# GpSimd hands weights' low parts, norm differences, residual sums, S5, rope and decay products to VectorE

## The chip, the cores and the metric

The kernel runs on one core of one Trainium2 chip. The core has TensorE (PE; its weight loads are listed as PEld), VectorE (DVE), ScalarE (ACT), GpSimd (POOL), and SyncE (SP), whose queue issues the DMAs. The metric is the device time of one execution in microseconds, as the median of several runs. TensorE's granted clock is given by the profile as a share of its upper level of 2.4 GHz; the lower level is 1.2 GHz.

## The reference

Two layers of a block over 1024 latent tokens and 256 context tokens of width 1024. In each layer the tokens are normalised and modulated, projected by one wide matrix into the columns of four mixers and their gates, mixed, gated, projected back and added to the stream. Cut to what matters here:

```python
for l in range(DEPTH):
    h = rmsnorm(x, g_pre[l]) * (1.0 + scale[:, None]) + shift[:, None]
    hc = rmsnorm(xc, g_pre[l]) * (1.0 + scale_c) + shift_c
    p_kv, p_q = jnp.split(h @ w_in[l], [N_CTX_COLS], axis=-1)
    ...
    y_gla, yc_gla = gla_mixer(...)      # linear attention with decays; rope on q and k
    y_na, yc_na = na_mixer(...)         # attention in an 8 x 16 window of a 2-D grid, and to the context
    y_s5, yc_s5 = s5_mixer(...)         # 16 groups of a diagonal state space model, two directions
    y_pool = pool_mixer(...)            # centred means over 2, 4, 8, 16 tokens
    y = jnp.concatenate([y_gla, y_na, y_s5, y_pool], axis=-1) * jax.nn.silu(gate_cols)
    x = x + gate[:, None] * rmsnorm(y @ w_out[l], g_post[l])
    # the context tokens likewise, except in the last layer
```

All of it is in float32.

## The kernel before

**Products in two parts.** TensorE gets each float32 operand as a high part (rounded) and a low part (the rest). `load_w` (L289) makes them for weights: a DMA brings a block of 128 x 1024 into the tile `w`, ScalarE rounds it into `wh` (L302), and another engine subtracts, `wl = w - wh` (L303). `norm_turn` (L268) does the same for the normalised tokens: `ahi` (L286) and `alo` (L287); `out_load` (L366) for the gated mixer outputs (L378 the gating, L381 the difference). Each product then is three series of matmuls: high by high, high by low, low by high. The weights' tiles lie in pools of three high parts, three low parts and two raw blocks, so a low part may be written only when the matmuls that read the tile three blocks ago are done. The output weights have tiles of their own (`wx`).

**Stages of a layer.** `norm_turn` prepares the tokens; `proj_tok` (L324, matmuls at L334) and `proj_cols` (L308, matmuls at L318) project them. `proj_gates` (L339) calls `proj_cols` for the output gates, applies a tanh and a product and stores the result in DRAM (L349). `s5_params` (L508) builds the state space matrices: per pair of groups complex products of 128 x 256 tiles, each made of products (L512 and, through `gmul`, L513) with a difference (L514) or a sum (L515); transposes by TensorE at L651 and small products at L656 and L657 read the results `sp_zr` and `sp_zi`, and `sp_R` is stored at L660. `gla_prep` (L862) rotates q and k (rope: a shuffle L893, a product with the sine L894, with the cosine L895, the sum L896), computes the decay gates (TensorE L901, VectorE L903), and sums them up (L915). `gla` (L990) subtracts the chunk's middle from the sums (L1001), clips (L1002), multiplies, reduces the largest decay to `glmx` (L1008), which TensorE transposes (L1010), and compares it with a limit (L1013). A branch on that flag (L1555) then takes the form with factored decays, which is the one that is run here; the other form never runs. The neighbourhood attention `na` (products L1315 and L1382, softmax L1322 to L1330), the pooling (L1434 to L1460) and the linear attention follow. Last comes the output: `out_load`, `out_mm` (matmuls L388), the squares, and `out_finish` (L447): the scaled rows (L474), the residual sum (L475), and, for the next layer's norm, a square with sum on ScalarE (L482) and the scaling (L483). The reciprocal root between them (L132 to L140) runs on VectorE.

**What sets the order.** Each engine runs its instructions in one fixed order. A scheduler sets it at build time by priorities and by the data each step needs, with its own idea of durations. The projections of the gates and of the pooling have low priority, so they fill TensorE's gaps; they stand on both sides of the branch, and what the scheduler has placed ahead of it can't fill behind it.

**Who does what.** A string `ENG` of 13 digits says for 13 kinds of elementwise work whether VectorE (1) or GpSimd (0) does it; `self.eng(i)` returns the engine.

## Time and profile before

| | us |
|---|---|
| median of 3 runs | 1439.78 |
| lowest, highest | 1434.55, 1441.52 |
| the profiled execution | 1441.78 |
| its span, first to last instruction | 1440.0 |
| TensorE busy | 1286.8 |
| VectorE busy | 898.0 |
| ScalarE busy | 585.0 |
| GpSimd busy | 414.0 |

The mean granted clock over the span is 0.951. The profiled execution lies 2.0 us above the median of the runs, and 1.8 us of it are outside the span. Busy time counts how long an engine had an instruction under way, also where that instruction was held up by another engine; so a busy share says nothing by itself about whether the engine could have done more. What bounds a stage is read from the waits: which engine stood idle, and whose result came last. Times within the span are counted from its first instruction. S5's products of layer 0 run from about 119 to 162 us, the output products of layer 0 come from about 690 on; S5's products of layer 1 are under way at 866, and the output products of layer 1 fill the time from 1380 on.

### The profile page before, as it was taken

What the parts mean: (1) busy time and instruction counts of PE and PEld (TensorE: products, weight loads), DVE (VectorE), ACT (ScalarE), POOL (GpSimd) and SP (SyncE); (2) the same over time, 40 slices, a digit from 0 to 9 for tenths busy, and PEclk for the clock granted to TensorE, in tenths of its full rate; (3) what the DMA queues carried; (4) which work ended last, traced back from release to release, by engine and by line L of the source; (5) the groups of instructions that cost most, each with busy time, mean ns of one, the idle gap of its engine ahead of it and who ended that gap; (6) DMA issues with size and microseconds to landing.
All of it is one profiled execution on the core that took longest, in us unless ns stands there. A gap on an engine that the chain in (4) does not pass through costs nothing. (4 is left out here: it accounts for less than half of the span.)

```text
span 1440.0 us, 20173 instructions
## 1 busy us (share of the span) xinstructions
PE 1286.8 (89%) x6958; PEld 1025.7 (71%) x6958; DVE 898.0 (62%) x2113; ACT 585.0 (41%) x1218; POOL 414.0 (29%) x368
## 2 busy tenths in 40 slices
PE   5798988999999899989999898888989989977897
PEld 2687956567777688767778877856867766765676
DVE  2878576555378557844654578385553894776473
ACT  2642433222333346733455642442233323665321
POOL 0215342010101033432654536331121110234351
PEclk9798999999999999989999998989999999988999
DMA  9445674762533277726842374655324535755662
GB/s 333 144 125 182 210 214 137 211 178 64 178 116 115 91 202 179 208 87 210 241 130 92 113 215 163 205 169 143 107 77 158 156 125 150 196 158 163 180 205 90
DMA packets 223479, 231.09 MB, mean 160 GB/s; under 512 B 47016, under 2 KB 176552, under 8 KB 223040
## 3 DMA queue, kind: packets, MB, share of 16 engines
q1 hardware_dynamic: 221776, 227.14, 52.3%
q10 hardware_dynamic: 1584, 2.49, 0.5%
q8 instruction: 59, 0.97, 0.3%
q14 instruction: 60, 0.49, 0.1%
HBM read 159.97 MB, written 69.62 MB: 159 GB/s over the span
## 5 line engine op out<-in xcount | busy, mean ns | idle before, releaser
L303 POOL TENSOR_TENSOR wl<-w,wh 128x1024 fp32r<-128x1024 f32 (+1 forms) x45 | 118.1, 2632 | 437.6 <-PE pa L318 197.1
L318 PE MATMUL pa<-ahi,wh 128*128 128x512 f32 (+1 forms) x664 | 175.2, 392 | 5.5 <-DVE stg L856 2.5
L318 PE MATMUL pa<-ahi,wl 128*128 128x512 f32 (+1 forms) x664 | 171.1, 385 | 0.4 <-PEq L1555 0.4
L318 PE MATMUL pa<-alo,wh 128*128 128x512 f32 (+1 forms) x664 | 168.2, 380 | 0.1
L318 PEld LDWEIGHTS pa<-ahi,wh 128*128 128x128 f32 x664 | 119.2, 198 | 34.5 <-issue 8.4
L318 PEld LDWEIGHTS pa<-ahi,wl 128*128 128x128 f32 x664 | 117.1, 195 | 28.9 <-issue 11.3
L318 PEld LDWEIGHTS pa<-alo,wh 128*128 128x128 f32 x664 | 115.8, 194 | 25.5 <-issue 7.5
L334 PE MATMUL pa<-wh,ahi 128*128 128x256 f32 (+1 forms) x480 | 84.8, 311 | 6.3 <-ACT wh L302 2.4
L388 PE MATMUL po<-wx,ahi 128*128 128x512 f32 x312 | 82.8, 407 | 4.8 <-ACT ahi L380 2.6
L334 PE MATMUL pa<-wl,ahi 128*128 128x256 f32 (+1 forms) x480 | 81.5, 304 | 2.5 <-POOL wl L303 2.5
L334 PEld LDWEIGHTS pa<-wh,ahi 128*128 128x128 f32 x480 | 70.2, 201 | 14.2 <-issue 5.4
L334 PE MATMUL pa<-wh,alo 128*128 128x256 f32 (+1 forms) x480 | 78.2, 300 | 0.0
L302 ACT CAST wh<-w 128x1024 fp32r<-128x1024 f32 (+1 forms) x51 | 53.7, 1056 | 57.3 <-PE pa L318 34.9
L1315 PE MATMUL nS<-naK,naQ 128*128 128x256 f32 (+2 forms) x256 | 58.8, 349 | 19.8 <-DVE nast L1322 17.3
L388 PEld LDWEIGHTS po<-wx,ahi 128*128 128x128 f32 x312 | 61.1, 197 | 19.5 <-ACT ahi L380 3.5
L334 PEld LDWEIGHTS pa<-wl,ahi 128*128 128x128 f32 x480 | 69.2, 199 | 5.8 <-POOL wl L303 3.0
L334 PEld LDWEIGHTS pa<-wh,alo 128*128 128x128 f32 x480 | 67.9, 197 | 1.7 <-issue 1.4
L1322 DVE CUSTOM_DVE_ANT_0 naP<-nS,nab 128x640 f32<-128x640 f32 (+1 forms) x64 | 50.2, 785 | 28.9 <-ACT nab L1273 14.8
L1315 PEld LDWEIGHTS nS<-naK,naQ 128*128 128x128 f32 x256 | 45.0, 204 | 32.0 <-DVE nast L1322 26.2
L198 PE MATMUL pm<-wm,csil 128*32 128x512 f32 x192 | 47.8, 679 | 19.0 <-DVE nr2v L132 9.5
L973 POOL TENSOR_TENSOR qs<-QB,ind 128x512 f32<-128x512 f32 x18 | 18.8, 1047 | 148.4 <-PE pb L1062 144.3
L1327 ACT ACTIVATE naP<-naP,nast 128x640 f32<-128x640 f32 (+1 forms) x64 | 51.5, 804 | 22.8 <-DVE nast L1322 17.5
(395 smaller groups left out, 2735.2 us busy)
## 6 DMA issues: line engine op xcount, KB each, us to landing
wm<-in_w_mod_dram SPq DMA_DIRECT2D x48, 512.0 KB
w<-in_w_in_dram SPq DMA_DIRECT2D x41, 512.0 KB
s5R<-dR SPq DMA_DIRECT2D x16, 960.0 KB
xt<-in_tok_dram SPq DMA_DIRECT2D x20, 512.0 KB
dR<-sp_R SPq DMA_DIRECT2D x16, 512.0 KB
dG<-stg SPq DMA_DIRECT2D x32, 256.0 KB
w<-in_w_out_dram SPq DMA_DIRECT2D x16, 512.0 KB
naQ<-dQ SPq DMA_DIRECT2D x24, 320.0 KB
```

Of the source, the lines that this page charges most:

```text
L198: nc.tensor.matmul(state[0][32 * k:32 * k + 32, :], lhsT=self.csil[:, (k0 + k) // 2, 2 * (k % 2):2 * (k % 2) + 32], rhs=ws[k // 2][:, k % ...
L302: nc.scalar.copy(hi, raw)
L303: (next(engines) if engines else self.eng(2)).tensor_tensor(lo, raw, hi.bitcast(F32), ALU.subtract)
L318: nc.tensor.matmul(ps[:, :t1 - t0], lhsT=w(k), rhs=x[:, k, t0:t1], start=(i == 0), stop=(i == 23))
L334: nc.tensor.matmul(ps[:, :n], lhsT=x[:, k, t * 128:(t + 1) * 128], rhs=w(k), start=(i == 0), stop=(i == 23))
L388: self.nc.tensor.matmul(o, lhsT=x[:, k], rhs=m(k), start=first and i == 0, stop=last and i == len(todo) - 1)
L973: (nc.gpsimd if BD[d] == "p" else nc.vector).tensor_tensor(out, Q.unsqueeze(1).to_broadcast(sh), ind.unsqueeze(2).to_broadcast(sh), ALU.mult)
L1315: nc.tensor.matmul(ps[:, c * 128:(c + n) * 128], lhsT=Qb[:, i, :], rhs=K[:, b * 128:(b + n) * 128], start=(i == 0), stop=(i == 1))
L1322: v.tensor_tensor_reduce(P[:, 0:nk], ps, bias[:, b0:b0 + nk], 1.0, -NEG, ALU.add, ALU.min, nm)
L1327: nc.scalar.activation(P[:, 0:nk], src, AF.Exp, bias=nm, scale=-1.0, accum_out=l1)
```

## The change

Six digits of `ENG` turn from 0 to 1: index 1 (the norm's `alo`, L287), 2 (the low parts of the weights, L303), 5 (the residual sum, L475), 6 (S5's `gmul`, L513), 10 (rope's sine product, L894) and 11 (the decay differences, L1001). `proj_cols` gets an argument with engines for `load_w`, and `proj_gates` passes GpSimd without end, so the low parts of the gates' weights stay there. Some low parts at the start of the program have had GpSimd or VectorE named for them before and are as they were.

```diff
-ENG = '0001000101001'
+ENG = '0111011101111'
...
-    def proj_cols(self, l, c0, n, evac, chunks, scale=None, psum=None):
+    def proj_cols(self, l, c0, n, evac, chunks, scale=None, psum=None, engines=None):
...
-            hi, lo = self.load_w(self.a["w_in"][l][:, c0 + m * 128:c0 + (m + 1) * 128], 128, scale=scale)
+            hi, lo = self.load_w(self.a["w_in"][l][:, c0 + m * 128:c0 + (m + 1) * 128], 128, scale=scale, engines=engines)
...
-        self.proj_cols(l, 1824 + m0 * 128, 128, evac, chunks, psum=psum)
+        self.proj_cols(l, 1824 + m0 * 128, 128, evac, chunks, psum=psum, engines=itertools.repeat(nc.gpsimd))
```

Of the instructions that are run, 156 move: 26 low parts of weights (24 of 128 x 1024, two of 128 x 1152), 20 norm differences, 34 residual sums, 64 products of S5, 8 of rope, 4 decay differences. VectorE's program has 3253 rows before and 3417 now, GpSimd's 555 and 391; eight of the 164 are rope products in the form that isn't run. The scheduler lays all engines' orders anew. Three places:

VectorE in S5 of layer 0, before. L512 is a product on VectorE, L514 and L515 the difference and the sum with a product `sp_big` that GpSimd makes.

```order
L512 TENSOR_TENSOR sp_zi_1290<-sp_zpr_1239,sp_bbi_1230 128x256
L512 TENSOR_TENSOR sp_R_1288<-sp_c2r_1263,sp_wpr_1241 128x2x128
L514 TENSOR_TENSOR sp_zi_1290<-sp_zi_1290,sp_big_1295 128x256
L514 TENSOR_TENSOR sp_R_1288<-sp_R_1288,sp_big_1299 128x2x128
L512 TENSOR_TENSOR sp_R_1288<-sp_c2i_1264,sp_wpr_1241 128x2x128
L515 TENSOR_TENSOR sp_R_1288<-sp_R_1288,sp_big_1300 128x2x128
L512 TENSOR_TENSOR sp_zr_1321<-sp_zpr_1239,sp_bbr_1229 128x256
L512 TENSOR_TENSOR sp_zi_1322<-sp_zpr_1239,sp_bbi_1230 128x256
```


VectorE at the same place, now:

```order
L513 TENSOR_TENSOR sp_big_1280<-sp_c2i_1264,sp_wpi_1242 128x256
L512 TENSOR_TENSOR sp_R_1269<-sp_c2i_1264,sp_wpr_1241 128x2x128
L514 TENSOR_TENSOR sp_R_1269<-sp_R_1269,sp_big_1280 128x2x128
L513 TENSOR_TENSOR sp_big_1281<-sp_c2r_1263,sp_wpi_1242 128x256
L512 TENSOR_TENSOR sp_zr_1289<-sp_zpr_1239,sp_bbr_1229 128x256
L515 TENSOR_TENSOR sp_R_1269<-sp_R_1269,sp_big_1281 128x2x128
L513 TENSOR_TENSOR sp_big_1291<-sp_zpi_1240,sp_bbi_1230 128x256
L512 TENSOR_TENSOR sp_zi_1290<-sp_zpr_1239,sp_bbi_1230 128x256
```


The products at L513 stand between the others, each ahead of the sum or difference that needs it.

VectorE at the end of S5 of layer 0 and ahead of the rope (L893), before. L1200 writes attention queries and keys.

```order
L515 TENSOR_TENSOR sp_R_1480<-sp_R_1480,sp_big_1492 128x2x128
L512 TENSOR_TENSOR sp_X_1532<-sp_i_321_1534,sp_dd_1089 16x256
L514 TENSOR_TENSOR sp_kc_1088<-sp_kc_1088,sp_X_1532 16x256
L514 TENSOR_TENSOR sp_T_320_1533<-sp_T_1530,sp_T_1531 128x2048
L1200 TENSOR_TENSOR stn_2795<-pa_2770,stn_2795 128x256
L893 STREAM_SHUFFLE QF_1560<-glk_1568 128x512
L893 STREAM_SHUFFLE KF_1561<-glq_1569 128x512
L1200 TENSOR_TENSOR stn_2833<-pa_2808,stn_2833 128x8x8x8
```


VectorE at the same place, now (`wl` is a low part; the fourth, `wl_3099`, gets the buffer of the first):

```order
L515 TENSOR_TENSOR sp_R_1480<-sp_R_1480,sp_big_1492 128x2x128
L303 TENSOR_TENSOR wl_2765<-w_2766,wh_2764 128x1024
L512 TENSOR_TENSOR sp_X_1532<-sp_i_321_1534,sp_dd_1089 16x256
L514 TENSOR_TENSOR sp_kc_1088<-sp_kc_1088,sp_X_1532 16x256
L303 TENSOR_TENSOR wl_2873<-w_2874,wh_2872 128x1024
L303 TENSOR_TENSOR wl_2979<-w_2980,wh_2978 128x1024
L1200 TENSOR_TENSOR stn_2795<-pa_2770,stn_2795 128x256
L514 TENSOR_TENSOR sp_T_320_1533<-sp_T_1530,sp_T_1531 128x2048
L1200 TENSOR_TENSOR stn_2833<-pa_2808,stn_2833 128x8x8x8
L303 TENSOR_TENSOR wl_3099<-w_3100,wh_3098 128x1024
L1200 TENSOR_TENSOR stn_2865<-pa_2840,stn_2865 128x8x8x8
L893 STREAM_SHUFFLE QF_1560<-glk_1568 128x512
```


Four low parts have come ahead of the first rope instruction.

TensorE at the end of the neighbourhood attention of layer 0 (its last product L1382) and ahead of the output products (L388), before. The L318 rows are gates' and other projections.

```order
L1382 MATMUL nT_9631<-naPT_9601,naV_9107 128x256 x3
L318 MATMUL pa_8229<-ahi,wl_8195 128x512 x8
L318 MATMUL pa_8258<-ahi,wh_8194 128x512 x8
L318 MATMUL pa_8258<-alo,wh_8194 128x512 x8
L318 MATMUL pa_8258<-ahi,wl_8195 128x512 x8
L318 MATMUL pa_8293<-ahi,wh_8287 128x256 x8
L318 MATMUL pa_8293<-alo,wh_8287 128x256 x8
L318 MATMUL pa_8293<-ahi,wl_8288 128x256 x8
L318 MATMUL pa_8322<-ahi,wh_8287 128x512 x8
L318 MATMUL pa_8322<-alo,wh_8287 128x512 x8
L318 MATMUL pa_8322<-ahi,wl_8288 128x512 x8
L318 MATMUL pa_9671<-ahi,wh_9665 128x512 x8
```


TensorE at the same place, now:

```order
L1382 MATMUL nT_9631<-naPT_9601,naV_9107 128x256 x3
L318 MATMUL pa_8322<-alo,wh_8287 128x512
L318 MATMUL pa_8322<-ahi,wl_8288 128x512 x8
L318 MATMUL pa_9671<-ahi,wh_9665 128x512 x8
L318 MATMUL pa_9671<-alo,wh_9665 128x512 x8
L318 MATMUL pa_9671<-ahi,wl_9666 128x512 x8
L388 MATMUL pa_9748<-wh_9710,stn_9499 128x512 x2
```


Of L318, 104 matmuls (24 with 256 columns) stood there and 33 stand now. The others have moved up: ahead of the branch of layer 0 there are 854 matmuls of L318 for 813 before, between it and the first attention product (L1315) 70 for 59, within the attention 195 for 176. In layer 1 it is 787 for 730 from the end of layer 0's attention to the branch, 53 for 49 behind it, and none for 61 within the attention.

## Rows read from the trace of the kernel before

**Rows 1.** The page's first part: busy us of each engine, share, instructions.

```profile
PE 1286.8 (89%) x6958; PEld 1025.7 (71%) x6958; DVE 898.0 (62%) x2113; ACT 585.0 (41%) x1218; POOL 414.0 (29%) x368
```

**Rows 2.** Waits of TensorE: line waiting <- line waited for: us, times, longest.

```profile
PE pb L651 <- DVE sp_zr L515: 11.0, 7, 4.0
...
PE pb L1010 <- DVE glmx L1008: 9.0, 2, 4.7
PE po L388 <- DVE stg L474: 8.5, 4, 3.2
...
PE pb L901 <- DVE QF L903: 3.5, 1, 3.5
...
PE pa L334 <- POOL wl L303: 2.5, 2, 1.8
```

**Rows 3.** Timeline in S5 of layer 0: start, us, engine, line, operation, [idle before].

```profile
130.48 2.52 POOL L303 TENSOR_TENSOR wl<-w,wh 128x1024 fp32r<-128x1024 f32 x1
130.72 2.56 DVE L515 TENSOR_TENSOR sp_zr<-sp_zr,sp_big 128x256 f32<-128x256 f32 x1
133.20 0.41 DVE L514 TENSOR_TENSOR sp_zi<-sp_zi,sp_big 128x256 f32<-128x256 f32 x1
...
133.42 0.45 PE L651 MATMUL pb<-c_ident,sp_zr 128*128 128x128 f32 x1 [3.60 <-DVE sp_zr L515]
```

**Rows 4.** Windows of 10 us: length, busy us of each engine, clock, DMA share, GB/s.

```profile
130.00:140.00 10.00, 6.58 (x31) 6.61 (x32) 8.21 (x12) 1.89 (x3) 4.49 (x4) 0.58 0.38 131
710.00:720.00 10.00, 6.89 (x26) 5.43 (x25) 7.81 (x22) 4.38 (x9) 6.83 (x6) 0.76 0.71 205
870.00:880.00 10.00, 6.42 (x34) 6.42 (x35) 8.28 (x11) 1.40 (x2) 4.73 (x5) 0.55 0.32 106
930.00:940.00 10.00, 3.93 (x18) 1.77 (x16) 8.80 (x11) 0.33 (x1) 5.68 (x3) 0.68 0.66 173
940.00:950.00 10.00, 8.83 (x30) 7.04 (x32) 8.46 (x15) 6.06 (x6) 2.52 (x2) 0.63 0.61 179
970.00:980.00 10.00, 5.64 (x23) 2.21 (x21) 7.25 (x10) 4.29 (x6) 0.00 (x0) 0.73 0.52 140
```

**Rows 5.** GpSimd by form: line, operation, tiles, count, busy, mean ns, idle before.

```profile
L303 POOL TENSOR_TENSOR wl<-w,wh 128x1024 fp32r<-128x1024 f32 x41 | 107.6, 2630 | 401.5 <-PE pa L318 197.1 <-ACT wh L302 149.3 <-DVE s5st L772 28.9
L475 POOL TENSOR_TENSOR xt<-xt,stg 128x512 f32<-128x512 f32 x34 | 45.4, 1356 | 46.3 <-DVE stg L474 37.9 <-issue 8.3
...
L287 POOL TENSOR_TENSOR alo<-nh,ahi 128x512 fp32r<-128x512 f32 x20 | 26.0, 1305 | 26.7 <-DVE ahi L286 23.6 <-DVE ry L140 2.3 <-DVE rv L132 0.4
...
L513 POOL TENSOR_TENSOR sp_big<-sp_zpi,sp_bbi 128x256 f32<-128x256 f32 x16 | 12.4, 778 | 25.9 <-DVE sp_R L514 19.6 <-DVE sp_bbi L514 6.3
...
L1001 POOL TENSOR_TENSOR QF<-glPF 128x1280 f32<-128x1280 f32 x2 | 6.0, 3014 | 19.8 <-DVE glPF L915 19.8
```

**Rows 6.** VectorE by form, the same columns.

```profile
L515 DVE TENSOR_TENSOR sp_zr<-sp_zr,sp_big 128x256 f32<-128x256 f32 x16 | 14.2, 885 | 2.6 <-POOL sp_big L513 2.6
...
L303 DVE TENSOR_TENSOR wl<-w,wh 128x1024 fp32r<-128x1024 f32 x6 | 7.3, 1218 | 9.1 <-PE pa L318 8.9 <-ACT wh L302 0.2
...
L265 DVE TENSOR_TENSOR alo<-nh,ahi 128x512 fp32r<-128x512 f32 x8 | 5.2, 685 | 0.1
```

**Rows 7.** Waits of the low parts on GpSimd and on VectorE.

```profile
POOL wl L303 <- PE pa L318: 197.1, 14, 33.6
...
DVE wx L303 <- ACT wx L302: 14.6, 8, 2.7
...
DVE wl L303 <- PE pa L318: 8.9, 2, 4.6
```

**Rows 8.** Timeline at an output turn of layer 0: residual sums, then the square.

```profile
706.04 3.04 POOL L475 TENSOR_TENSOR xt<-xt,stg 128x512 f32<-128x512 f32 x2
...
709.12 1.06 ACT L482 ACTIVATE stn<-xt 128x1024 f32<-128x1024 f32 x1 [2.38 <-POOL xt L475]
```

**Rows 9.** The chain that ended last: start, us, line, number.

```profile
1380.72 50.87 PE po L388 x216
```


## The prediction

> **What bounds the kernel now.** I read the page's first line, then TensorE's waits, then the windows with its granted clock, then the instructions of GpSimd and VectorE by form. The first line [rows 1] says that TensorE (PE) is busy for 1286.8 of the 1440.0 us of the span, VectorE (DVE) for 898.0 and GpSimd (POOL) for 414.0. So TensorE bounds the kernel, with some 153 us of idle time, and the change can only win a part of that idle time, and the time that TensorE spends at a low clock. Work taken off GpSimd is worth nothing by itself.
>
> Which of TensorE's waits end at something that the change touches? Five lines do [rows 2]: the S5 transposes at L651 waiting for a product that needs one of GpSimd's (11.0 us in 7 waits), the GLA transposes at L1010 waiting behind the decay differences (9.0 in 2), the output products at L388 (8.5 in 4), the gate products at L901 (3.5), and L334 waiting for a low part (2.5). Together 34.5 us. The others (DMA, the softmax of the neighbourhood attention) are not touched.
>
> Why is L651 late? [rows 3] shows it: GpSimd starts a low part of 2.52 us at 130.48, VectorE's product sp_zr starts at 130.72 and takes 2.56 us, though the like product right behind it takes 0.41, and the TensorE transpose that needs it has waited 3.60 us. Both end together: VectorE's two-operand product stood still while GpSimd's ran. The windows [rows 4] show the second price: after such waits the granted clock is lower, 0.58 at 130 to 140 and 0.55 at 870 to 880 (S5 of the two layers), 0.68, 0.63 and 0.73 around GLA of layer 1, 0.76 at an output wait. Between the levels of 1.2 and 2.4 GHz, a mean of 0.58 with 6.58 us busy means that about (1 - 0.58) x 6.58 = 2.8 us of work at full clock was not done. The six rows give 2.8 + 2.9 (S5), 1.3 + 3.3 + 1.5 (GLA), and 1.7 (output) us: 13.5 in all.
>
> **What is moved, and its bare cost.** From GpSimd go 26 low parts of weights at 2.63 us, 34 residual sums at 1.36, 20 norm differences at 1.31, 64 S5 products at 0.78, 4 decay differences at 3.0 [rows 5], and 8 rope products, which have the size of the norm differences: about 68 + 46 + 26 + 50 + 12 + 10 = 212 us of its 414. On VectorE a low part takes 1.22 and a 128x512 difference 0.685 [rows 6], a 128x256 product 0.41 when nothing is beside it [rows 3]; the decay difference is estimated by size, 1280/512 x 0.685 = 1.71. So it gets 26 x 1.22 + 64 x 0.41 + 62 x 0.685 + 4 x 1.71 = 107 us, and wins back some of what it lost beside GpSimd: 16 products at L515 at 0.885 [rows 6] instead of 0.41 are 8 us. It comes to about 1000 us, 69% of the span, below TensorE: in the mean VectorE does not become the bound. In a stretch it may.
>
> **(a) S5 products: -13.** Per pair of groups, VectorE issues a product, waits for GpSimd's, and adds. On one engine there is no hand-over and no product standing still: four 0.41 instead of four 0.78 on another engine. Bounds: 0 if the transposes find another late input, and 11.0 + 5.7 (clock) = 16.7 if all goes. I take 9 of 11.0, since one or two of the seven waits are likely to come from the loop's own length, which VectorE now carries alone, and 4 of 5.7 with them.
>
> **(b) Decay differences and rope: -12.** The order moves output-gate products of TensorE ahead of the branch: in layer 0, 41 matmuls of 512 columns, in layer 1, 57. In the steady part at the end 216 such take 50.87 us [rows 9], 0.236 each, so 9.7 and 13.5 us of work now stand where TensorE waited 9.0 us in two waits. Those waits should go (-9). On VectorE itself the chain is about as long as before: the eight rope products and four differences add 8 x 0.685 + 4 x 1.71 = 12.3 us to it, but no hand-over and no standing still are left. Of L901's 3.5 and the clock's 6.1 I take 3. Bounds: 0 (the chain grows by what it wins) and 18.6.
>
> **(c) Residual, norm, weights in the output stage: -6.** At an output turn two residual sums take 3.04 us on GpSimd, the square on ScalarE (L482) waits 2.38 us for them [rows 8], and VectorE, in order, waits for that square with the next tile's scaling behind it, for which L388 waits. Two sums on VectorE are 1.37 us, 1.7 less, for each of the four waits of 8.5: some 4 of them, as a shorter wait leaves its rest. L334's 2.5 for a low part: 2 go. Bounds: 0 and 8.5 + 2.5 + 1.7 = 12.7.
>
> **(d) Cover given back: +8.** The gate products that fill the waits in (b) are the ones that stood elsewhere. Behind the last attention product of layer 0 there were 104 (24 of them half as wide), now 33: 71 x 0.236 = 17 us less to do while the attention's last tiles are normalised, stored and read back for the output stage. The attention of layer 1 keeps none of the 61 it had. What of the 17 us was needed there no row tells; bounds are 0 and 17, and I take the middle.
>
> **(e) Low parts on the in-order VectorE: +4.** A low part waits for the cast on ScalarE and for the buffer that TensorE frees. On GpSimd such waits were free: 197.1 us in 14 for the buffer [rows 7]. On VectorE everything behind waits too. The rows that show it there are the output weights (14.6 us in 8, 1.8 each) and 8.9 in 2 for a buffer. Bounds: 0 if all falls into VectorE's slack (TensorE waited for no VectorE low part so far), and 26 x 1.8 = 47 if all reaches TensorE. I take one wait of the longer kind (4.5), rounded to 4, since VectorE has 440 us of slack.
>
> Sum: -13 - 12 - 6 + 8 + 4 = -19. On the profiled execution, 1441.8, this gives 1422.8; that execution lies 2.0 above the median of 1439.8, so **1421** is forecast.
>
> **Rivals.** *The standing still remains (no change).* GpSimd keeps 17 low parts of the gates, the gating products of the output stage and the pooling; a moved product that starts beside one of these stands still as in [rows 3], 2.56 - 0.41 = 2.15 us at a low part. If each of the 17 meets one, and half of it reaches TensorE, that is 17 x 2.15 / 2 = 18 us: 1439. For it: the gates' low parts are filler, spread over just these stretches. Against it: in (a) and (b) VectorE no longer waits for GpSimd's result itself. The Trainium skill, SBUF — State Buffer, "Who interferes with whom", says that the two engines share a port pair by an exclusive lock, so that the later one stops fully, whichever it is; it speaks for this rival, and the trace agrees (2.56 beside 0.41 us).
>
> *VectorE's queue blocks (slower).* Place: ahead of the rope in both layers. In the new order four low parts, the last with the buffer that the first must leave, stand ahead of the first rope instruction. If that buffer is still being read, VectorE waits with rope, scans and differences behind it. The mean wait for such a buffer was 197.1 / 14 = 14.1 us [rows 7]. If the whole of it is exposed in both layers, 28 us come on top, (b)'s 12 are not won, and the cover's loss is 17, not 8: 1422.8 + 28 + 12 + 9 - 2 = 1470; with half the wait exposed, 1456. It outweighs the gains once over (19 - 12) / 2 = 3.5 us per layer are exposed. Against it: the fill that frees the buffer also keeps TensorE busy until then. The Trainium skill, TensorE: Matmul & The Clock Gate (its opening table), lists VectorE's queue as strictly first in, first out; the trace agrees, since the waits on VectorE in [rows 7] let nothing pass.
>
> *All of it goes (faster still).* All five waits and the lost clock, with nothing given back: 1441.8 - 34.5 - 13.5 - 2 = 1392.
>
> That the change does less than it says is excluded: the order has 164 rows more on VectorE and as many less on GpSimd.
>
> **How the numbers follow.** Forecast (1405 to 1433) 0.55; no change (1433 to 1447) 0.18; slower (about 1447 to 1470) 0.15; faster still (1392 to 1405) 0.12. A run of this kernel can be told from no change at about 0.5%, 7 us. So faster 0.66 (the forecast and the last, less a little of the forecast's edge), same 0.19, slower 0.15. The range of 1392 to 1452 leaves out most of the blocked queue and little else.
>
> **What would show it.** (a) the line L651 <- sp_zr falls below 3 us, and the clock at S5 in both layers stays above 0.9; products at L512 and L515 take about 0.41. (b) L1010 <- glmx falls to near nothing; if the line grows, the queue blocks. (c) L388 <- stg halves. (d) a new TensorE wait between the attention of layer 0 and its output products, or in the attention of layer 1. (e) new lines "wl L303 <- PE" on VectorE, and TensorE waiting for VectorE low parts. I am wrong if TensorE's busy time at full clock changes by more than a few us, or if the gain is in stages where no row above has a wait.

## The result and the profile after

The changed kernel takes 1390.53 us in the median (1389.38 to 1392.13, 4 runs); the kernel before took 1440.65 beside it. The ratio is 0.9653, with a 95% interval of 0.9627 to 0.9679: 50 us faster, where 19 were forecast, and 1.5 us below the lower end of the range of 1392 to 1452. For the kernel below with the weights back, median and ratio are of seven executions, without three of 1444 to 1446 us that lie over 1.5% above its fastest; a loss of 44 us that an expectation names for it is from the median of all ten.

The first part of the page, after (engine, busy us, share of the span, instructions), beside [rows 1]:

```profile
span 1388.7 us, 20066 instructions
...
PE 1265.2 (91%) x6958; PEld 1011.0 (73%) x6958; DVE 912.5 (66%) x2269; ACT 584.9 (42%) x1218; POOL 203.8 (15%) x212
```

Three numbers here tell the case. TensorE has the same 6958 matmuls, but is busy for 1265.2 us and not 1286.8: 21.6 us less, which is the clock (its mean went from 0.951 to 0.968). Its idle time, span less busy, went from 153.2 to 123.5: 29.7 us less. The two are the 51.3 us by which the span got shorter. And GpSimd's busy time fell by 210.2 us, close to the 212 that the prediction had moved, but VectorE's rose by 14.5 us only, from 898.0 to 912.5, though 156 instructions came to it.

What these instructions take on VectorE, from the same kernel's rows by form (line, operation, tiles, count, then busy us and mean ns of one):

```profile
L303 DVE TENSOR_TENSOR wl<-w,wh 128x1024 fp32r<-128x1024 f32 x30 | 37.2, 1242 | 27.7 <-ACT wh L302 17.4 <-PE pa L318 10.3
...
L303 DVE TENSOR_TENSOR wl<-w,wh 128x1152 fp32r<-128x1152 f32 x2 | 2.6, 1356 | 2.2 <-ACT wh L302 2.2
...
L475 DVE TENSOR_TENSOR xt<-xt,stg 128x512 f32<-128x512 f32 x34 | 25.2, 780 | 0.0
...
L287 DVE TENSOR_TENSOR alo<-nh,ahi 128x512 fp32r<-128x512 f32 x20 | 13.8, 691 | 1.2
...
L381 DVE TENSOR_TENSOR alo<-yt,ahi 128x512 fp32r<-128x512 f32 x24 | 20.2, 847 | 11.9 <-ACT ahi L380 11.5
...
L286 DVE CAST ahi<-nh 128x512 fp32r<-128x512 f32 x20 | 8.5, 425 | 11.1 <-ACT nh L280 11.1
...
L513 DVE TENSOR_TENSOR sp_big<-sp_zpi,sp_bbi 128x256 f32<-128x256 f32 x16 | 6.6, 414 | 0.1
...
L515 DVE TENSOR_TENSOR sp_zr<-sp_zr,sp_big 128x256 f32<-128x256 f32 x16 | 6.6, 413 | 0.0
...
L1001 DVE TENSOR_TENSOR QF<-glPF 128x1280 f32<-128x1280 f32 x2 | 2.9, 1472 | 0.0
...
L894 DVE TENSOR_TENSOR QF<-QF,rs 128x512 f32<-128x512 f32 x4 | 2.8, 690 | 0.5 <-DMA rs<-in_rope_s_dram 0.5
```

Low parts: 37.2 less the 7.3 of the six that were there before [rows 6], and 2.6 for two of 128x1152, are 32.5. Residual sums 25.2, norm 13.8, the four forms of L513 6.6 each, rope 5.6, decay 5.9: 109.4 us in all, for 107 predicted. So 898.0 + 109.4 - 912.5 = 94.9 us of VectorE's busy time have gone. Most of that was no work: the durations of the 2113 instructions that VectorE had before add up to 84.4 us less now. The other 10.5 us come from the way of counting, since the records of neighbouring instructions overlap by some 45 ns each, and a new one adds less than its duration. L515's 16 sums take 413 ns and not 885 [rows 6]; and operations that the change does not touch got shorter in the same way. Before, by form:

```profile
L381 DVE TENSOR_TENSOR alo<-yt,ahi 128x512 fp32r<-128x512 f32 x24 | 23.0, 959 | 19.2 <-ACT ahi L380 18.7
...
L140 DVE SCALAR_TENSOR_TENSOR ry<-rw,ry 128x1 f32<-128x1 f32 x84 | 21.6, 270 | 1.1
...
L286 DVE CAST ahi<-nh 128x512 fp32r<-128x512 f32 x20 | 16.1, 811 | 14.7 <-ACT nh L280 14.7
...
L895 DVE TENSOR_TENSOR glq<-glq,rc 128x512 f32<-128x512 f32 x4 | 5.9, 1486 | 0.0
```

L381 went from 959 to 847 ns, L286 from 811 to 425; of the other two, after:

```profile
L140 DVE SCALAR_TENSOR_TENSOR ry<-rw,ry 128x1 f32<-128x1 f32 x84 | 14.7, 183 | 1.0
...
L895 DVE TENSOR_TENSOR glq<-glq,rc 128x512 f32<-128x512 f32 x4 | 2.8, 690 | 0.0
```

L140 works on one number per partition and L895 on 512. The trace before shows beside what they were long. Of L140's 84 executions, the 31 that overlap an operation of GpSimd (fills not counted) took 466 ns on the mean, the other 53 took 155 and none over 160. For L895 it is 1557 ns (6) and 680 (2), and for the cast L286, which has one operand only, 1067 (12) and 426 (8). The product ahead of L140, with one tile and two numbers per partition as operands (`rw`, L136), is not drawn out: 270 ns (30) and 269 (54). So a good part of VectorE's work stood still while GpSimd worked, though not all kinds of it.

TensorE's waits after (us, times, longest), to hold beside [rows 2]:

```profile
PE po L388 <- DVE stg L474: 6.3, 4, 3.7
...
PE pb L901 <- DVE QF L903: 2.2, 1, 2.2
...
PE pm L198 <- DMA wm<-in_w_mod_dram: 0.8, 2, 0.7
...
PE pb L651 <- DVE sp_zi L514: 0.7, 1, 0.7
...
PE pb L1010 <- DVE glmx L1008: 0.6, 2, 0.3
```

L651's 11.0 us are 0.7 (for the other product), L1010's 9.0 are 0.6, L901's 3.5 are 2.2, L388's 8.5 are 6.3, and L334's line for the low part on GpSimd is gone. One line went that was not counted, of before:

```profile
PE pm L198 <- DMA wm<-in_w_mod_dram: 9.5, 3, 4.5
```

The waits for the modulation's weights went from 9.5 to 0.8 us. Between S5's last transposes and the first L198, TensorE's order has 123 matmuls of L318 now and had 65 (131 and 87 in layer 1), so it comes to L198 with more done, when the data have landed. No run tests that by itself.

By stage, windows of before: S5 of layer 0, then from S5's end to L1010 (rope and decays), the output stage to S5 of layer 1, S5 and rope of layer 1 (us, then busy us of each engine, granted clock, DMA share, GB/s):

```profile
126.50:161.00 34.50, 29.70 (x218) 28.80 (x216) 30.51 (x54) 9.72 (x22) 21.12 (x27) 0.85 0.54 182
161.00:223.50 62.50, 52.02 (x288) 40.52 (x288) 38.37 (x61) 27.02 (x39) 21.14 (x10) 0.95 0.64 193
641.00:864.30 223.30, 206.61 (x1035) 175.28 (x1034) 127.61 (x354) 107.96 (x223) 100.69 (x75) 0.96 0.54 164
864.30:900.80 36.50, 29.78 (x221) 28.18 (x219) 32.22 (x58) 9.87 (x22) 22.41 (x29) 0.86 0.50 168
900.80:976.20 75.40, 63.30 (x332) 49.65 (x331) 47.06 (x69) 33.06 (x46) 24.41 (x11) 0.90 0.61 180
```

and after:

```profile
125.10:155.20 30.10, 29.42 (x253) 29.19 (x251) 29.78 (x86) 9.31 (x22) 0.00 (x0) 1.00 0.57 198
155.20:220.50 65.30, 62.41 (x353) 50.33 (x352) 43.00 (x76) 31.59 (x46) 0.00 (x0) 1.00 0.77 223
628.80:827.00 198.20, 189.99 (x964) 161.10 (x963) 134.28 (x393) 104.34 (x216) 26.15 (x22) 0.98 0.56 173
827.00:859.30 32.30, 32.16 (x276) 31.90 (x274) 32.12 (x93) 9.50 (x23) 0.00 (x0) 1.00 0.57 196
859.30:925.10 65.80, 64.06 (x324) 49.67 (x324) 44.24 (x77) 31.48 (x45) 0.00 (x0) 1.00 0.77 223
```

In S5 TensorE now has hardly any idle time in either layer (0.7 and 0.1 us for 4.8 and 6.7), and the clock is at its upper level throughout (1.00 for 0.85 and 0.86). The same in the rope stage: idle 2.9 and 1.7 for 10.5 and 12.1, clock 1.00 for 0.95 and 0.90. The output stage is 25 us shorter. GpSimd does nothing at all in four of these five windows; of the gates' low parts that stayed with it, none lies there.

The attention stages gave some of it back. Before:

```profile
517.20:641.00 123.80, 111.81 (x695) 94.58 (x694) 93.61 (x235) 76.58 (x179) 52.41 (x69) 0.96 0.63 170
1222.30:1340.40 118.10, 95.12 (x552) 79.47 (x553) 83.48 (x202) 68.22 (x150) 41.93 (x56) 0.90 0.60 163
```

and after:

```profile
500.80:628.80 128.00, 113.36 (x712) 95.63 (x713) 98.87 (x240) 78.85 (x183) 55.46 (x71) 0.97 0.62 174
1175.30:1289.80 114.50, 84.03 (x491) 69.54 (x491) 81.35 (x199) 65.74 (x145) 41.66 (x56) 0.90 0.59 157
```

TensorE's idle time there is 14.6 and 30.5 us; it was 12.0 and 23.0.

### The profile page after: what moved, and what is told of

Its sections match the earlier page's. It is cut to its first block, busy times and chain, and to the rows that moved or that the text cites. A ratio compares the mean times of both kernels' runs of the same rounds, so it can differ in the third digit from the quotient of the medians.

```text
span 1388.7 us, 20066 instructions
## 1 busy us (share of the span) xinstructions
PE 1265.2 (91%) x6958; PEld 1011.0 (73%) x6958; DVE 912.5 (66%) x2269; ACT 584.9 (42%) x1218; POOL 203.8 (15%) x212
## 5 line engine op out<-in xcount | busy, mean ns | idle before, releaser
L318 PE MATMUL pa<-ahi,wh 128*128 128x512 f32 (+1 forms) x664 | 171.7, 387 | 5.0 <-ACT stg L1407 2.1
L318 PE MATMUL pa<-alo,wh 128*128 128x512 f32 (+1 forms) x664 | 166.9, 380 | 0.1
L318 PE MATMUL pa<-ahi,wl 128*128 128x512 f32 (+1 forms) x664 | 165.1, 377 | 0.1
L318 PEld LDWEIGHTS pa<-ahi,wh 128*128 128x128 f32 x664 | 116.0, 193 | 31.8 <-issue 6.4
L318 PEld LDWEIGHTS pa<-alo,wh 128*128 128x128 f32 x664 | 115.7, 192 | 25.7 <-issue 7.9
L318 PEld LDWEIGHTS pa<-ahi,wl 128*128 128x128 f32 x664 | 115.6, 191 | 23.5 <-issue 5.5
L334 PE MATMUL pa<-wh,ahi 128*128 128x256 f32 (+1 forms) x480 | 83.4, 305 | 5.8 <-ACT wh L302 2.4
L303 POOL TENSOR_TENSOR wl<-w,wh 128x1024 fp32r<-128x1024 f32 (+1 forms) x19 | 46.3, 2441 | 286.0 <-PE pa L318 170.8
L388 PE MATMUL po<-wx,ahi 128*128 128x512 f32 x312 | 79.8, 396 | 1.1 <-DVE stg L474 1.0
L334 PE MATMUL pa<-wl,ahi 128*128 128x256 f32 (+1 forms) x480 | 79.6, 299 | 0.1
L1315 PE MATMUL nS<-naK,naQ 128*128 128x256 f32 (+2 forms) x256 | 61.2, 359 | 19.8 <-DVE nast L1322 17.8
L334 PEld LDWEIGHTS pa<-wh,ahi 128*128 128x128 f32 x480 | 68.8, 197 | 11.4 <-issue 3.3
L334 PE MATMUL pa<-wh,alo 128*128 128x256 f32 (+1 forms) x480 | 76.0, 294 | 0.0
L334 PEld LDWEIGHTS pa<-wl,ahi 128*128 128x128 f32 x480 | 68.1, 195 | 6.6 <-issue 5.3
L1315 PEld LDWEIGHTS nS<-naK,naQ 128*128 128x128 f32 x256 | 46.0, 209 | 32.9 <-DVE nast L1322 28.1
L388 PEld LDWEIGHTS po<-wx,ahi 128*128 128x128 f32 x312 | 59.2, 191 | 14.7 <-DVE stg L474 1.4
L334 PEld LDWEIGHTS pa<-wh,alo 128*128 128x128 f32 x480 | 65.7, 193 | 5.7 <-issue 5.5
L1382 PE MATMUL nT<-naPT,naV 128*128 128x256 f32 (+3 forms) x368 | 53.4, 284 | 7.9 <-DVE naPT L1367 5.4
L973 POOL TENSOR_TENSOR qs<-QB,ind 128x512 f32<-128x512 f32 x18 | 19.2, 1066 | 275.4 <-PE pb L1062 159.8
```

The source lines that it names most:

```text
L303: (next(engines) if engines else self.eng(2)).tensor_tensor(lo, raw, hi.bitcast(F32), ALU.subtract)
L318: nc.tensor.matmul(ps[:, :t1 - t0], lhsT=w(k), rhs=x[:, k, t0:t1], start=(i == 0), stop=(i == 23))
L334: nc.tensor.matmul(ps[:, :n], lhsT=x[:, k, t * 128:(t + 1) * 128], rhs=w(k), start=(i == 0), stop=(i == 23))
L388: self.nc.tensor.matmul(o, lhsT=x[:, k], rhs=m(k), start=first and i == 0, stop=last and i == len(todo) - 1)
L973: (nc.gpsimd if BD[d] == "p" else nc.vector).tensor_tensor(out, Q.unsqueeze(1).to_broadcast(sh), ind.unsqueeze(2).to_broadcast(sh), ALU.mult)
L1315: nc.tensor.matmul(ps[:, c * 128:(c + n) * 128], lhsT=Qb[:, i, :], rhs=K[:, b * 128:(b + n) * 128], start=(i == 0), stop=(i == 1))
```

## Experiments

Most kernels differ from the two known ones only by digits of `ENG` (index from 0: 1 norm, 2 weights, 4 gating, 5 residual, 6 S5, 10 rope, 11 decay); the gates' low parts stay on GpSimd unless said otherwise. Each was timed in three rounds beside the kernel before, whose median was 1438.6 to 1442.1 in these rounds.

| kernel | us, median | ratio to before, 95% |
|---|---|---|
| changed, S5 back | 1404.06 | 0.9751 (0.9712 to 0.9790) |
| changed, weights back | 1430.69 | 0.9940 (0.9905 to 0.9974) |
| changed, norm and residual back | 1407.29 | 0.9770 (0.9731 to 0.9809) |
| changed, rope and decay back | 1395.54 | 0.9672 (0.9627 to 0.9716) |
| before, weights alone moved | 1415.86 | 0.9841 (0.9817 to 0.9865) |
| before, S5 alone | 1431.72 | 0.9950 (0.9931 to 0.9969) |
| before, norm and residual alone | 1438.98 | 1.0011 (0.9989 to 1.0033) |
| before, rope and decay alone | 1441.17 | 1.0011 (0.9994 to 1.0029) |
| before, weights and S5 | 1405.00 | 0.9761 (0.9722 to 0.9801) |
| before, weights, norm and residual | 1420.80 | 0.9850 (0.9810 to 0.9890) |
| changed, GpSimd reads in S5 | 1430.19 | 0.9932 (0.9901 to 0.9963) |
| changed, GpSimd fills in S5 | 1403.17 | 0.9756 (0.9703 to 0.9808) |
| changed, gates' low parts moved too | 1387.53 | 0.9653 (0.9632 to 0.9675) |
| changed, gating moved too | 1376.40 | 0.9569 (0.9552 to 0.9585) |
| the same, gates' low parts too | 1378.81 | 0.9564 (0.9525 to 0.9604) |
| the same, nearly all on VectorE | 1401.27 | 0.9724 (0.9695 to 0.9753) |

**One part put back.** Theory A was that each part pays by its own hand-over between the engines; theory B that the long low parts on GpSimd hold VectorE up.

```diff
-ENG = '0111011101111'
+ENG = '0111010101111'
...
+ENG = '0101011101111'
...
+ENG = '0011001101111'
...
+ENG = '0111011101001'
```

S5:

> The changed kernel with S5's 64 products back on GpSimd, all else as changed. Theory A (hand-over between the engines in each pair of groups): the S5 stages lose what they had won, some 15 to 21 us, so 1405 to 1412 us, and the line L651 <- sp_zr is back at 8 us or more. Theory B (the long low parts of weights on GpSimd are what held VectorE's products): with these gone S5 on GpSimd costs little, 1391 to 1397 us, and L651 <- sp_zr stays below 4 us.

Weights:

> The changed kernel with the weights' 26 low parts back on GpSimd. Theory A: these low parts are filler, they cost a few us in GLA's preparation alone: 1393 to 1400 us. Theory B (each low part holds VectorE's two-operand work for 2.6 us): over half of the 50 us goes, 1415 us or more, and VectorE's products in S5 and GLA show durations of 1.5 to 2.5 us again.

Norm and residual:

> The changed kernel with the norm differences and the residual sums back on GpSimd. Theory A: the output stage of layer 0 loses what it had won, 7 to 13 us: 1397 to 1404 us, in L388 <- stg and in the low clock there. Theory B: they matter only beside low parts on GpSimd: 1390 to 1394 us.

Rope and decay:

> The changed kernel with the rope products and the decay differences back on GpSimd. Theory A (hand-over in the chain from rope to glmx): 10 to 20 us are lost: 1400 to 1410 us, with waits at L1010. Theory B: without low parts on GpSimd beside them they cost 0 to 5 us: 1390 to 1396 us.

The weights cost most: putting them back takes 40 us of the 50. S5 costs 13.5, norm and residual 16.8, rope and decay 5.0, so S5 and norm come out near A's ranges (a little below the one, above the other), the weights and rope in B's. Together they make some 75 us, more than there is. Either parts make each other worse, or the order, which the scheduler lays anew each time, has its own effect.

The kernel with the weights back does not show what theory B expected of it. In its trace, of an execution of 1446.4 us, VectorE's products in S5 of layer 0 are short. GpSimd is the one that stands still. Its row there, of the timeline (start, us, engine, line, operation):

```profile
126.50 22.84 POOL L303 TENSOR_TENSOR wl<-w,wh 128x1024 fp32r<-128x1024 f32 x1 [5.65 <-ACT wh L302]
```

A low part that takes 2.63 us on the mean takes 22.84 beside VectorE's dense row of two-operand products. TensorE waits once in that stage, for 5.7 us; so how the 40 us come about is not shown.

**One part alone.** The same four, from the other side.

```diff
-ENG = '0001000101001'
+ENG = '0011000101001'
...
+ENG = '0001001101001'
...
+ENG = '0101010101001'
...
+ENG = '0001000101111'
```

Weights:

> The kernel before with the weights' 26 low parts alone on VectorE (the gates' stay on GpSimd). Theory B (the low parts on GpSimd are the main cause, as the loss of 44 us by putting them back suggests): 1400 to 1412 us, and the 2.5 us products in S5 are gone. Theory C (the 44 us come from the interplay with S5 on VectorE, where GpSimd's low part starves beside a dense row of products; alone the low parts are worth less): 1415 to 1430 us.

S5:

> The kernel before with S5's products alone on VectorE; the weights' low parts stay on GpSimd. Theory B: 1425 to 1432 us, the 13 us that undoing it cost. Theory C: no gain or a loss, 1435 to 1450 us, and a low part on GpSimd that begins in an S5 stage takes 10 us or more instead of 2.6, since VectorE's products leave it no gap.

Norm and residual:

> The kernel before with the norm differences and residual sums alone on VectorE. If they are worth by themselves what undoing them cost (17 us): 1420 to 1426 us. If most of it came from the order that is laid anew, or only without low parts on GpSimd: 1432 to 1440 us. The output stage alone should be 7 to 10 us shorter in either case.

Rope and decay:

> The kernel before with the rope products and decay differences alone on VectorE. By the prediction's step on them: 1425 to 1432 us. By what undoing them cost (5 us), since the low parts on GpSimd still hold up the chain: 1432 to 1442 us.

Weights 23 us, S5 7, the other two nothing: 30 of the 50. For the weights that is theory C of the expectation, which takes the 44 us for an interplay. For S5 the time lies in B's range; but its trace shows C's sign, a low part on GpSimd that is drawn out at the start of each S5 stage, though by less than the 10 us that C named. Layer 0 and layer 1:

```profile
125.72 7.38 POOL L303 TENSOR_TENSOR wl<-w,wh 128x1024 fp32r<-128x1024 f32 x1 [6.36 <-ACT wh L302]
```

```profile
866.62 7.70 POOL L303 TENSOR_TENSOR wl<-w,wh 128x1024 fp32r<-128x1024 f32 x1 [5.68 <-ACT wh L302]
```

The expectation of 7 to 10 us in the output stage from the norm and residual alone failed: that stage went from 223.3 to 221.2 us.

**Pairs.** Do parts make each other worse?

```diff
-ENG = '0001000101001'
+ENG = '0011001101001'
...
+ENG = '0111010101001'
```

Weights and S5:

> The kernel before with the weights' low parts and S5's products on VectorE, the other two parts on GpSimd. Alone they were worth 23 and 7 us. If they hold each other up, the pair is worth more than 30: 1395 to 1407 us. If each has its own price, 1408 to 1412 us.

Weights, norm and residual:

> The kernel before with the weights' low parts, the norm differences and the residual sums on VectorE; S5, rope and decay stay on GpSimd. Alone they were worth 23 and 0 us. If they hold each other up in the output stage, where both lie: 1400 to 1410 us. If each has its own price: 1414 to 1418 us.

Weights and S5 together reach 0.9761; the product of their single ratios is 0.9841 x 0.9950 = 0.979, within the interval, so the pair adds at most a little. Weights with norm and residual are worth what the weights are alone, just outside the expected range. Yet with weights and S5 there, adding norm and residual is worth some 10 us (1405.0 to 1395.5). So it isn't pairs with the weights that make 50 of 30; where the rest comes from these runs do not settle.

**Reading and filling.** The disputed mechanism by itself. The two kernels have the same order on TensorE, VectorE, ScalarE and the DMA queue; GpSimd does extra work in S5 that nothing uses. In both, a copy of one column first waits for a product of VectorE, so that hand-over is the same.

```diff
                     cmul(z_r, z_i, e8(zr), e8(zi), e16(bbr), e16(bbi), sh, "big", gmul)
+                    dm = pt("dm", (128, 1024))
+                    nc.gpsimd.tensor_copy(dm[:, 0:1], z_r.rearrange("p g t h -> p (g t h)")[:, 0:1])
+                    nc.gpsimd.tensor_tensor(dm, self.ahi[:, 0, 0:1024].bitcast(F32), self.ahi[:, 1, 0:1024].bitcast(F32), ALU.subtract)
...
+                    nc.gpsimd.memset(dm, 0.0)
+                    nc.gpsimd.memset(dm, 0.0)
```

Reads:

> The changed kernel, and in each of S5's 16 pairs GpSimd makes one 128x1024 difference of two tiles in SBUF that nothing uses (about 2.6 us alone). If VectorE's two-operand products and GpSimd's reads exclude each other, either some of VectorE's products take 2.5 us, 16 x 2.1 = 34 us in all, or GpSimd's take 10 to 20 us: S5's stages get 5 to 15 us longer each, 1400 to 1420 us. If it was the hand-over of results alone that cost time: as the like kernel with fills, within 3 us.

Fills:

> The same kernel, with the same order on the other engines, but GpSimd writes zeros to the tile twice (about 2 us) and reads nothing. If reads exclude each other, fills cost nothing: 1388 to 1396 us, and VectorE's products take 0.41 us. If any work on GpSimd disturbs VectorE: as the kernel with reads.

Reading costs 27 us more than filling. Both times missed the expected ranges, 1430 for 1400 to 1420 and 1403 for 1388 to 1396; the difference between them is what the pair was made for. Two of VectorE's forms in S5, a difference and a sum, with the reads:

```profile
L514 DVE TENSOR_TENSOR sp_zi<-sp_zi,sp_big 128x256 f32<-128x256 f32 x16 | 17.5, 1094 | 0.0
L515 DVE TENSOR_TENSOR sp_R<-sp_R,sp_big 128x256 f32<-128x256 f32 x16 | 17.4, 1087 | 0.1
```

and the same two with the fills:

```profile
L514 DVE TENSOR_TENSOR sp_zi<-sp_zi,sp_big 128x256 f32<-128x256 f32 x16 | 6.7, 421 | 0.0
...
L515 DVE TENSOR_TENSOR sp_R<-sp_R,sp_big 128x256 f32<-128x256 f32 x16 | 6.7, 420 | 0.1
```

With the fills each takes 0.42 us, as in the changed kernel (0.41); with the reads 1.09 us on the mean. That mean is made of two kinds: with the reads just 16 of S5's products of 128x256 take 2.5 to 2.6 us, one for each difference on GpSimd, and the other 188 at most 0.44. Apart from that the kernels are alike: the extra work keeps GpSimd busy for 73 us with the reads and for 67 with the fills, and VectorE's products wait for no result of GpSimd in either. S5 of layer 0 with reads (a window as above):

```profile
124.80:169.00 44.20, 36.34 (x252) 35.12 (x250) 44.01 (x90) 9.37 (x22) 30.54 (x14) 0.85 0.29 108
```

and with fills:

```profile
124.70:154.00 29.30, 29.30 (x253) 29.11 (x251) 28.93 (x83) 9.31 (x22) 27.67 (x18) 1.00 0.43 163
```

44.2 us for 29.3, and TensorE idle for 7.9 us and at a clock of 0.85, as in the kernel before; in layer 1 it is 48.1 for 32.4. The 30.6 us in the two stages are the whole difference and a little more. So it is GpSimd's reading that holds up VectorE's two-operand work, and this alone, with the same hand-over and the same order, costs what was measured. GpSimd is held up in turn; a copy of one column takes 2.3 us on the mean beside these products (with the fills, line, tiles, count, busy, mean):

```profile
L634 POOL COPY sp_dm<-sp_zr 128x1 f32<-128x1 f32 x16 | 36.2, 2262 | 8.0 <-DVE sp_zr L515 7.2
```

The kernel with fills is still 12.6 us slower than the changed one, though its S5 stages are as short. Its order differs from that of the changed kernel, and the loss appears where GpSimd has no extra work: from L1010 to the first attention product of layer 0 it takes 299 us for 281. So the order is the likely cause; no run tests it by itself. The differences of 5 to 17 us above, between kernels with other orders, carry an uncertainty of that size.

**Further in the same direction.** What is left on GpSimd is moved as well: the gates' low parts; the gating products (the string also sets indices 0 and 8, which nothing reads, so the spreading at L973, which the expectation names, stayed on GpSimd); both; and then the spreading and the pooling.

```diff
-        self.proj_cols(..., engines=itertools.repeat(nc.gpsimd))
+        self.proj_cols(...)
...
-ENG = '0111011101111'
+ENG = '1111111111111'
...
-BD = 'ap'
+BD = 'av'
...
-                gp.tensor_tensor(s2[:, 1:W], u[:, 0:W - 1], u[:, 1:W], ALU.add)
+                nc.vector.tensor_tensor(s2[:, 1:W], u[:, 0:W - 1], u[:, 1:W], ALU.add)
...
```

Gates' low parts:

> The changed kernel with the gates' 17 low parts on VectorE as well. If what is left on GpSimd still holds VectorE up: faster by 3 to 10 us, 1380 to 1388 us. If these low parts stand where VectorE has no dense work, and on VectorE's queue their waits for buffers (on GpSimd over 100 us) hold up what stands behind: slower, 1395 to 1420 us, with TensorE waiting for VectorE in the linear attention and the neighbourhood attention.

Gating:

> The changed kernel with the gating products of the output stage (L378) and the spreading in the linear attention (L973) on VectorE too; the gates' low parts stay on GpSimd. If mutual holding is what is left in the output stage: 1378 to 1388 us. If VectorE's order is what bounds that stage now (its sums and differences already stand there in a row): 1388 to 1400 us.

Both:

> The kernel with the gating products on VectorE too (1376 us), and now the gates' low parts as well. If every two-operand operation left on GpSimd costs VectorE: 1366 to 1374 us. If the gates' low parts on VectorE's queue cost what they win, as in the kernel with them alone: 1374 to 1382 us.

And nearly everything:

> The same, and the spreading in the linear attention and the pooling on VectorE too, so that GpSimd has next to nothing. If the gain goes on: below 1366 us, with VectorE's operations at their shortest everywhere. If VectorE's own load now bounds the neighbourhood attention, where the pooling lies: 1376 to 1395 us, with more waits of TensorE for VectorE there.

The gates' low parts make no difference that can be told. The gating products are worth 14 us more, and that kernel, 1376.4 us, beats both of its expected ranges. Its output stage:

```profile
626.20:813.90 187.70, 182.89 (x953) 156.01 (x952) 132.34 (x407) 101.57 (x213) 2.29 (x4) 1.00 0.59 181
```

187.7 us for 198.2, at a clock of 1.00, and L381 takes 685 ns for 847: the operation that follows each gating product no longer stands still. With nearly everything on VectorE the time goes back to 1401, above the expected 1376 to 1395. The two attention stages with it:

```profile
506.10:649.50 143.40, 126.81 (x735) 104.55 (x735) 122.42 (x311) 82.42 (x185) 0.42 (x4) 0.94 0.59 163
1177.50:1300.60 123.10, 91.01 (x493) 76.72 (x493) 98.28 (x251) 65.40 (x144) 0.21 (x2) 0.83 0.52 140
```

They take 143.4 and 123.1 us, for 128.0 and 114.5 in the changed kernel, and VectorE is busy there for 122.4 and 98.3 us, for 98.9 and 81.4. No operation of VectorE is drawn out any more, but its own load is what counts there. The pooling lies in these stages, which speaks for leaving it on GpSimd; the spreading was moved along with it, and no run parts the two.

The excess of VectorE's busy time puts the runs on one scale. It is worked out from the rows by form: for each form, the busy time less the count times the shortest mean that this form has in any of these kernels. Before it is 123 us. With rope and decay moved alone it is 114, norm and residual 117, S5 98, weights 97, weights and S5 75, all four parts 42, the gating too 32, the gates too 12, nearly everything 5. In this order the times, down to 32, are 1440, 1441, 1439, 1432, 1416, 1405, 1390, 1376. That is a trend and no law: S5 alone and the weights alone have the same excess and lie 16 us apart, and most kernels not named here lie within some 10 us of the row. Two fall out of it. The reads have 82 us at 1430: in S5, 30 us of excess more than with the fills (52) cost 27 us, while from before to the changed kernel 81 us of excess went for 50 us. The kernel with the weights back has 74 us in its trace, at 1431; there a low part on GpSimd was the one held up. Below 32 the row ends, since VectorE's load grows.

## Why the prediction was right and wrong

**Right in kind, far too small.** VectorE did stand still beside GpSimd, TensorE did wait for it, and moving the work ended most of that. The likeliest case said 1421. What came, 1390.5, is near the 1392 of the rival "all of it goes", which had a chance of 0.12, but that is luck. Of that rival's five waits, 34.5 us, some 25 went, and cover was given back in the attention stages; what made up for it is a wait that the prediction had put at nothing (L198) and more clock than it had counted.

**The step that failed: the sizes of (a), (b) and (c).** The gains were added up from five lines of TensorE's waits and six windows of low clock, and all other waits were taken as untouched. The prediction's own measure can be taken over the whole stages from the windows shown above: TensorE's idle time, and (1 - clock) x busy time for the clock. The second is an estimate, good to some 2 us, since the clock is given to two digits.

| term, layers together | forecast | its bound | idle time, fall | clock, fall | together |
|---|---|---|---|---|---|
| (a) S5 | 13 | 16.7 | 10.7 | 8.6 | 19 |
| (b) rope and decays | 12 | 18.6 | 18.0 | 8.9 | 27 |
| (c) output | 6 | 12.7 | 8.5 | 4.5 | 13 |
| (d) attention | -8 | -17 | -10.1 | 2.2 | -8 |
| (e) VectorE's queue | -4 | -47 | no line | | 0 |

Gains are positive. So the first three make 59 us where 31 were forecast (with (d), about the whole 51.3 us of the span), and (a) and (b) lie above the upper bounds that the prediction gave them. The largest miss is (b): its idle time fell not only at the two lines it counted (L1010 by 8.4 us, L901 by 1.3), but also by 8.7 us of DMA waits at L198.

**Behind it: what VectorE wins back.** For VectorE's load the prediction had 107 us of new work and 8 us won back, from the 16 sums at L515 alone. The new work measures 109; the old instructions got 84 us shorter. The one form with the plainest name was taken for the whole effect. The rows to see it by were there: in [rows 6] a 128x512 difference with nothing beside it takes 685 ns, and the like difference at L381 had a mean of 959; the cast at L286 had 811, and 426 where GpSimd did nothing beside it. Such pairs of rows, summed over the forms, would have put tens of us where the prediction had 8, and in the rope and output stages too.

**(a) S5, -13: too small.** Idle time in the two stages fell by 4.1 and 6.6 us, 10.7 in all, above the 9 that were taken; the clock came on top of that, with 1.00 for 0.85 and 0.86 over the whole stages, some 8.6 us, where 4 us were taken from two windows of 10 us. The run with S5 back loses 13.5 us, the one with S5 alone gains 7; a size for this part alone is not to be had from them, since the order differs in each.

**(b) Rope and decays, -12: too small, for two reasons.** The fill ahead of the branch did what was said: L1010's 9.0 us are 0.6. The chain on VectorE, which was to be as long as before, is so in layer 0: from the first shuffle to glmx 35.4 us before and 35.3 after. In layer 1 it is not. Its ends, before:

```profile
931.21 0.72 DVE L893 STREAM_SHUFFLE QF<-glk 128x512 f32<-128x512 f32 x1
...
935.47 2.83 DVE L896 TENSOR_TENSOR glk<-glk,QF 128x512 f32<-128x512 f32 x1
...
958.01 2.37 DVE L997 TENSOR_TENSOR glrg<-glPF 128x10 f32<-128x10 f32 x1
...
975.62 0.18 DVE L1008 TENSOR_REDUCE glmx<-glrg 128x1 f32<-128x40 f32 x1
```

and after:

```profile
889.12 0.74 DVE L893 STREAM_SHUFFLE QF<-glk 128x512 f32<-128x512 f32 x1
...
924.57 0.18 DVE L1008 TENSOR_REDUCE glmx<-glrg 128x1 f32<-128x40 f32 x1
```

44.6 us have become 35.6. Before, low parts and the decay differences on GpSimd lay in the midst of it, and six of VectorE's operations were drawn out by some 10 us together: L896 took 2.83 us for 0.69 after, L997 2.37 for 0.17, a scan at L915 2.55 for 0.40, L996 1.72 for 0.16, and two products at L895 1.42 and 1.74 for 0.69. What came to the chain on VectorE cost less than that: four products, two decay differences and a low part, 6.9 us together. And the DMA waits of L198, 8.7 us, were said to be untouched and went.

**(c) Output, -6: too small.** The stage from the last attention product of layer 0 to S5 of layer 1 is 25 us shorter, of which TensorE's idle time makes 8.5 (16.7 to 8.2). L388's wait for the scaled rows, from which the step was built, fell by 2.2 us only (8.5 to 6.3), for 4 expected; it did not halve, as the sign for (c) asked. The rest is other waits, the clock (0.98 for 0.96), and fill done elsewhere. That the gating products hold the same stage up the prediction did not see; moving them too made the kernel 14 us faster, 10.5 of them in this stage.

**(d) Cover given back, +8: the size about right, by luck.** TensorE's idle time in the two attention stages rose by 2.6 and 7.5 us. The 8 was half of 17 us at the end of layer 0's attention, which is the smaller part; the larger is layer 1's, which lost all its fill and was given no price. The 17 itself was too high: of the 71 matmuls 24 are half as wide, which makes it 59 x 0.236 = 13.9 us, and the half 7.

**(e) Low parts in VectorE's queue, +4: not seen.** The waits came on VectorE, 10.3 us in 4 for a buffer and 19.5 in 7 for a cast, for 8.9 in 2 and next to nothing before. But TensorE has no line for a low part on VectorE, and the four low parts ahead of the rope hardly delayed it: from S5's end to the first shuffle it is 29.6 us for 26.7 in layer 0 and 29.8 for 30.4 in layer 1. The rival of the blocked queue is out. Its break-even of 3.5 us per layer was wrong too: with (b) not won and 9 us more cover lost, as it says itself, the sum is a small loss before any wait is exposed.

**The clock.** Six windows were priced at 13.5 us, of which the forecast took at most 7. The same matmuls take 21.6 us less in all, beside 29.7 us of idle time. By the table, most of it lay in the S5 and rope stages, over their whole length and not in single windows.

**The rival of standing still that remains** had the mechanism, but priced it for the wrong operations: the gates' low parts cost nothing measurable (1387.5 for 1390.5; none lies in S5 or in the rope stage), the gating products of the output stage do (14 us).

**What stays open.** That GpSimd's reading holds VectorE up, and what it costs in S5, is shown by the pair of reads and fills. How the 50 us divide between this and the new order is not: a kernel with another order, and GpSimd's fills, lost 12.6 us, and single parts sum to 30 from one side and to some 75 from the other. Why the waits at L198 went, and how the weights put back cost 40 us, is open as well.

## What to carry to other kernels

Before work is put on GpSimd beside a busy VectorE, compare the mean of VectorE's forms with the shortest mean of the same shape: the excess, summed over the forms, is what sharing costs VectorE, and here it was 123 us of 898. What it costs the kernel depends on the stage: nearly all of it where VectorE's row is dense and TensorE waits for it, as in S5 with the reads, and less elsewhere. Moving work to one engine then costs that engine far less than the sum of its durations, 14.5 us for 109 in this case, and it pays as long as that engine does not become the bound of the stage, as VectorE did with the pooling. When idle time on TensorE is priced, add the clock of the whole stage, and do not call a wait untouched because the change has no line in it: here 0.7 us of clock came with each us of idle time won, and 8.7 us with the DMA waits at L198.

## What the runs showed of the hardware

That the standing still goes both ways was not expected. In one execution a low part on GpSimd, 2.63 us on the mean, took 22.84 us beside VectorE's dense two-operand products, which kept their 0.41 us each; in another kernel two took 7.4 and 7.7, and a copy of one column took 2.3 us on the mean. Fills on GpSimd do not disturb VectorE (421 ns beside them, 413 without), reads do: one product of 2.5 to 2.6 us for each difference, 1.09 us on the mean in two forms. VectorE's smallest operations are held like the large ones: L140, on one number per partition, took 466 ns beside GpSimd's work and 155 otherwise. And it is not two-operand work alone: the cast at L286 took 1067 ns and 426, while the product at L136, with one tile as operand, took 270 and 269. The Trainium skill, SBUF — State Buffer, "Who interferes with whom", states that a two-operand operation of VectorE contends with a GpSimd instruction that reads SBUF and not with one that only writes it; the pair of reads and fills agrees.
